# Moving 14 of 31 convolution shifts of the odd mixer from TensorE and VectorE to ScalarE and accumulating DMAs

## The chip, the cores and the metric

The kernel runs on one core of one Trainium2 chip. The metric is the device time of one execution in microseconds (us), the median of several runs.

## The reference, cut to what matters

A trunk of two layers on 512 tokens of width 1024, all in float32. Layer 0 has an attention mixer (even), layer 1 a mixer of a spatial gating unit and a causal convolution (odd):

```
for layer in 0, 1:
    h += 1/2 swiglu(rms(h));  h += Mixer_layer(rms(h));  h += 1/2 swiglu(rms(h))
    h += sigmoid(rms(h) @ ple_wgate[layer]) * (p[layer] @ ple_wproj[layer])     # p: 512 x 256, ple_wproj: 256 x 1024

odd mixer:
    zc, zd = split(xn @ w_in)                      # w_in: 1024 x 2048
    u, v = split(gelu(zc));  v = layer_norm(v)
    c_out = u * (block_mix(v) + bias)
    a, g = split(zd);  hd = a * sigmoid(g)         # 512 tokens x 512 channels
    y[t, c] = d_conv_b[c] + sum over shifts s = 0..30 of d_conv_w[30 - s, c] * hd[t - s, c]
    d_out = silu(layer_norm(y))
    mix = concat(c_out, d_out) @ w_out             # w_out: 1024 x 1024
```

## The kernel before

Activations are held with channels on the 128 partitions and the 512 tokens along the row, so one tile of 128x512 floats (256 KB) is a block of 128 channels. A big product is computed from two halves of each operand: a value is split into `hi` (a copy rounded to the type fp32r) and `lo` (what is left), and `mm3` makes three passes on TensorE, hi*hi, hi*lo, lo*hi. A plain `mm` on float32 tiles is one call that TensorE runs as several passes; the profile shows two rows for each call.

Weights come in units of 1 MB: SP issues the load into one of two `raw` buffers, ScalarE casts it to `whi` (L297), VectorE subtracts to get `wlo` (L321), and TensorE uses the pair.

Nothing is issued in the order of the code. Every operation is first recorded in a plan. `order()` then places them one by one with fixed costs for each operation, a bias for each stream of work (`CONV_BIAS`, `PP_BIAS` and so on: a larger bias makes a stream yield), and a limited number of buffers of each kind (`SLOTS`: 28 `a` buffers, 12 `t` buffers of 128x512) and of each kind in a stream (`CAPS`). What comes out is one fixed instruction sequence for each engine. On the chip each engine works its sequence off strictly in order, and waits at an instruction until its inputs and its buffer are ready.

The work of the odd mixer around the change, in `odd_mixer`: the products for `zd` give `hds`, four tiles of `hd` (ct = 0 to 3). Then the products for v, then those for u, run on TensorE; beside them VectorE works on the convolution. Of the 31 shifts, `PE_TAPS` = 4 are matmuls of `hds[ct]` with a diagonal matrix that ScalarE makes from the identity (stream `convp`), and the other 27 are `stt` operations on VectorE (L330), one for each shift and ct, that accumulate in `ys[ct]`. After the gating unit the first half of the product with w_out runs, and among its matmuls the tail of the convolution (`dtail`) starts: `mm(p, ones, ys[i])` sums the channels for the layer norm. The last half of w_out needs the normed `ys`.

`ple_proj(1)`, the product p[1] @ ple_wproj[1] for the end of layer 1, is also placed in the odd mixer (stream `pp`): 16 `mm` calls on float32, whose results are stored to DRAM (`pp<-t`) and read back at the end.

Of the kernel before, what the change touches and what calls it, by code (L numbers as in the profile page):

```python
# [257 lines left out]
def trunk(ctx: ExitStack, tc: tile.TileContext, A: dict, out: bass.AP):  # L258
# [89 lines left out]

    def gdma(o, x):
        P.op("POOL", 1000.0, lambda: nc.gpsimd.dma_start(ap(o), ap(x)), w=[o], r=[x, box.get("gate")], lat=2500.0)  # L350
# [32 lines left out]
    class Unit:  # L383


        def __init__(self, srcs, k, cols, by_cols):
            raw = P.tile("raw", (128, k, cols))
            for c0, c1, src in srcs:
                dma(raw[:, :, c0:c1], src, 0.5 * k * (c1 - c0))
            self.by_cols, self.half = by_cols, cols // 2 if by_cols else (k + 1) // 2  # L390
            h = self.half
            self.split([raw[:, :, h * i:h * (i + 1)] if by_cols else raw[:, h * i:h * (i + 1), :] for i in range(2)])
# [33 lines left out]
    def wunit(w, k0, k, c0, cols):  # L426
        src = w[128 * k0:128 * (k0 + k), c0:c0 + cols].rearrange("(k p) c -> p k c", p=128)
        return Unit([(0, cols, src)], k, cols, k == KD)
# [158 lines left out]
    def ffn(pre, layer, norm, nxt, hook=None, first=None):  # L587
        xs, rcol, rb = norm.finish()
        wg, wu, wd = A[pre + "_wg"][layer], A[pre + "_wu"][layer], A[pre + "_wd"][layer]
        for j0, j1 in ((0, 6), (6, 11)):  # L590
            cats = []
            for j in range(j0, j1):
# [5 lines left out]
                if hook is not None and j == 7:  # L598
                    box["gate"] = cats[-1][0]
                    with P.on("hook", HOOK_BIAS):  # L600
                        hook()
# [34 lines left out]
    def ple_proj(layer, after):  # L636
# [11 lines left out]
        for mg in range(2):  # L648
            wp = [at() for _ in range(2)]
            for k in range(2):  # L650
                dma(wp[k], A["ple_wproj"][layer, 128 * k:128 * k + 128, 512 * mg:512 * mg + 512], 256, after)
            for i in range(4):
                p = ps()
                for k in range(2):
                    x, y = (wp[k], pT[k]) if layer == 0 else (pT[k], wp[k])
                    mm(p, x[:, 128 * i:128 * i + 128], y, k == 0, k == 1)
                c = tt()
                acopy(c, p)
                d = dram_tile(f"pp{layer}{mg}{i}")
                dma(d, c, 256)  # L660
                kept.append(d)
# [111 lines left out]
    def even_mixer(norm, nxt, cos, sin):  # L773
# [198 lines left out]
        with P.on("pp", PP0_BIAS):  # L972
            box[0] = ple_proj(0, bqk[7])
# [85 lines left out]
    def odd_mixer(norm, nxt, consts):  # L1059
# [21 lines left out]
        with P.on("convp", CONVP_BIAS):  # L1081

            for ct in range(4):
                p = ps()
                for i in range(PE_TAPS):
                    dg = tt(shape=(128, 128))
                    act(dg, ident, AF.Copy, scale=cvw[:, 4 * (last - i) + ct:4 * (last - i) + ct + 1])
                    mm(p[:, i:S], dg, hds[ct][:, 0:S - i], i == 0, i == PE_TAPS - 1)
                y = at()
                act(y, p, AF.Identity, bias=vcol[:, 17 + ct:18 + ct])  # L1090
                ys.append(y)
        with P.on("conv", CONV_BIAS):
            for ct in range(4):
                y = ys[ct]
                for i in range(last - PE_TAPS, -1, -1):
                    sh = last - i
                    stt(y[:, sh:S], hds[ct][:, 0:S - sh], cvw[:, 4 * i + ct:4 * i + ct + 1], y[:, sh:S], OP.mult, OP.add)
# [111 lines left out]
    def odd_consts_hook():  # L1209
# [15 lines left out]
    ffn("ffn2", 1, n, m)  # L1225
# [11 lines left out]
TOPK_BIAS, AQ_BIAS, CONV_BIAS, CONVP_BIAS, PP_BIAS, DTAIL_BIAS, HOOK_BIAS, PE_TAPS = 2000, 450, 3000, -300, 200, -300, 400, 4  # L1237
PP0_BIAS = 600
PAD = 416
# [30 lines left out]
```

## Time and profile before

| | |
|---|---|
| median of 3 runs | 2010.78 us (2010.63 to 2011.23) |
| the profiled execution: its time, its span | 2010.54 us, 2008.6 us |
| TensorE (PE) busy | 1991.3 us, 99% of the span |
| VectorE (DVE) busy | 1080.8 us, 54% |
| ScalarE (ACT) busy | 723.2 us, 36% |
| GpSimd (POOL) busy | 13.8 us, 1% |
| granted TensorE clock | 0.999 |

The span runs from the first to the last instruction of the trace; 1.9 us of the execution's time lie outside it. Matmuls are pipelined, so the busy time of TensorE counts a matmul row until its modelled end; how long one takes when many follow each other is read from the starts of neighbouring rows. The odd mixer lies between 1428 and about 1604 us of the span.

### The profile page before, as it was taken

The numbers are of one execution on the slowest core, as the hardware profiler recorded it, in microseconds if no ns is written. First come the engines' busy times: TensorE is split into PE (matmuls) and PEld (weight loads), VectorE is DVE, ScalarE is ACT, GpSimd is POOL, SyncE is SP. The second block draws the span as 40 slices with busy tenths as digits, with TensorE's granted clock in tenths as the row PEclk, the third lists the DMA queues.
The fourth block names the chain that finished last, engine by engine and source line by source line (L and its number), as shares of the span: only waits on it lengthen the run. The fifth ranks groups of instructions, "written<-read, shape, count | busy, mean of one in ns | idle before, by whom it ended". The sixth has DMA issues, their size and how long they took to land.

```text
span 2008.6 us, 22735 instructions
## 1 busy us (share of the span) xinstructions
PE 1991.3 (99%) x9154; PEld 1630.2 (81%) x9154; DVE 1080.8 (54%) x1797; ACT 723.2 (36%) x1057; POOL 13.8 (1%) x35
## 2 busy tenths in 40 slices
PE   8999999999999999999999999999999999999999
PEld 7888888888767888888888888888767888888887
DVE  6442464489986544344466443444699744334443
ACT  6322233344756422132254222223425533213232
POOL 0000000000000000000000000000000000000000
PEclk9999999999999999999999999999999999999999
DMA  5323322354330323332233322323333232323222
GB/s 189 105 97 98 108 85 84 94 160 141 96 110 22 104 86 105 94 95 95 95 121 110 105 98 92 105 75 103 107 105 105 84 97 92 105 85 104 95 104 75
DMA packets 164778, 202.28 MB, mean 101 GB/s; under 512 B 9968, under 2 KB 123072, under 8 KB 164672
## 3 DMA queue, kind: packets, MB, share of 16 engines
q1 hardware_dynamic: 164016, 200.38, 31.3%
q8 instruction: 72, 1.18, 0.2%
q0 software_dynamic: 528, 0.41, 0.2%
q14 instruction: 34, 0.28, 0.0%
q10 hardware_dynamic: 128, 0.03, 0.0%
HBM read 185.33 MB, written 6.29 MB: 95 GB/s over the span
## 4 chain that ended last, share of the span: by engine, by line
PE 97%; DVE 1%; ACT 1%; DMA 1%; issue 0%; SPq 0%; ACTq 0%; DVEq 0%
PE ps L281 30%; PE ps L282 30%; PE ps L283 30%; PE ps L276 6%; PE ps L287 1%; DMA whi<-in_x_dram 0%; ACT t L292 0%; ACT t L297 0%; DVE t L962 0%; DVE t L330 0%; DVE wlo L330 0%; DMA t<-t 0%; DVE t L309 0%; DVE wlo L321 0%; DVE a L913 0%
## 5 line engine op out<-in xcount | busy, mean ns | idle before, releaser
L297 ACT CAST whi<-raw 128x1024 fp32r<-128x1024 f32 (+2 forms) x342 | 348.7, 1022 | 976.3 <-PE ps L282 936.7
L321 DVE TENSOR_TENSOR wlo<-raw,whi 128x1024 fp32r<-128x1024 f32 (+2 forms) x342 | 405.1, 1185 | 496.8 <-ACT whi L297 496.0
L281 PE MATMUL ps<-x,whi 128*128 128x512 f32 x1664 | 655.8, 394 | 0.6 <-ACT x L297 0.6
L282 PE MATMUL ps<-x,whi 128*128 128x512 f32 x1664 | 648.7, 390 | 0.6 <-DVE x L321 0.6
L283 PE MATMUL ps<-x,wlo 128*128 128x512 f32 x1664 | 648.8, 390 | 0.0
L281 PEld LDWEIGHTS ps<-x,whi 128*128 128x128 f32 x1664 | 313.1, 188 | 66.2 <-ACT x L297 1.1
L283 PEld LDWEIGHTS ps<-x,wlo 128*128 128x128 f32 x1664 | 312.9, 188 | 65.6
L282 PEld LDWEIGHTS ps<-x,whi 128*128 128x128 f32 x1664 | 313.2, 188 | 65.1 <-DVE x L321 1.2
L281 PE MATMUL ps<-a,whi 128*128 128x512 f32 x832 | 325.1, 391 | 0.0
L282 PE MATMUL ps<-a,whi 128*128 128x512 f32 x832 | 323.9, 389 | 0.0
L283 PE MATMUL ps<-a,wlo 128*128 128x512 f32 x832 | 323.8, 389 | 0.0
L281 PEld LDWEIGHTS ps<-a,whi 128*128 128x128 f32 x832 | 156.3, 188 | 32.8 <-issue 0.5
L283 PEld LDWEIGHTS ps<-a,wlo 128*128 128x128 f32 x832 | 156.2, 188 | 32.6
L282 PEld LDWEIGHTS ps<-a,whi 128*128 128x128 f32 x832 | 156.2, 188 | 32.3 <-DVE a L321 0.7
L315 DVE TENSOR_TENSOR t<-ps,t 128x512 f32<-128x512 f32 x88 | 60.8, 691 | 209.1 <-PE ps L283 208.3
L315 DVE TENSOR_TENSOR t<-ps,rb 128x512 f32<-128x512 f32 x100 | 68.7, 687 | 112.1 <-PE ps L283 109.9
L330 DVE SCALAR_TENSOR_TENSOR a<-a 128x508 f32<-128x508 f32 (+23 forms) x108 | 72.7, 731 | 5.0 <-ACT a L292 4.6
L292 ACT ACTIVATE t<-t 128x512 f32<-128x512 f32 x100 | 62.9, 629 | 22.9 <-DVE t L315 22.8
L297 ACT CAST a<-t 128x512 fp32r<-128x512 f32 x88 | 54.8, 623 | 36.8 <-DVE t L315 36.8
L315 DVE TENSOR_TENSOR t<-t,rb 128x512 f32<-128x512 f32 x92 | 63.2, 687 | 1.2
L321 DVE TENSOR_TENSOR a<-t,a 128x512 fp32r<-128x512 f32 x88 | 60.4, 686 | 5.2 <-ACT a L297 4.8
L276 PE MATMUL ps<-a 128*128 128x512 f32 (+3 forms) x152 | 58.6, 501 | 1.5 <-ACT t L297 0.5
(167 smaller groups left out, 1358.8 us busy)
## 6 DMA issues: line engine op xcount, KB each, us to landing
raw<-in_ffn_wg_dram SPq DMA_DIRECT2D x43, 1024.0 KB, 5.1
raw<-in_ffn_wu_dram SPq DMA_DIRECT2D x43, 1024.0 KB, 5.1
raw<-in_ffn_wd_dram SPq DMA_DIRECT2D x40, 1024.0 KB, 4.9
raw<-in_ple_wgate_dram SPq DMA_DIRECT2D x8, 1024.0 KB, 5.0
raw<-in_od_w_in_dram SPq DMA_DIRECT2D x8, 1024.0 KB, 5.5
raw<-in_ev_w_in_dram SPq DMA_DIRECT2D x7, 1024.0 KB, 5.8
raw<-in_ffn_wd_dram SPq DMA_DIRECT2D x8, 512.0 KB, 3.7
raw<-in_ev_w_out_dram SPq DMA_DIRECT2D x4, 1024.0 KB, 5.3
```

Of the source, the lines that this page charges most:

```text
L276: P.op("PE", cost, lambda: nc.tensor.matmul(ap(p), ap(a), ap(b), start=start, stop=stop), w=[p], r=[a, b], lat=160.0)
L281: nc.tensor.matmul(q, x, u, start=first, stop=False)
L282: nc.tensor.matmul(q, x, v, start=False, stop=False)
L283: return nc.tensor.matmul(q, y, u, start=False, stop=last)
L287: P.op("PE", 107.0, lambda: nc.tensor.transpose(ap(p), ap(x), ap(idn)), w=[p], r=[x, idn], lat=160.0)
L292: P.op("ACT", cost, lambda: nc.scalar.activation(ap(o), ap(x), func, scale=ap(scale), bias=ap(bias), **({"accum_out": ap(accum)} if accum ...
L297: P.op("ACT", 0.83 * o.n + (52.0 if x.psum else 93.0), lambda: nc.scalar.copy(ap(o), ap(x)), w=[o], r=[x])
L315: dve(o, lambda: nc.vector.tensor_mul(ap(o), ap(a), ap(b)), [a, b])
L321: dve(o, lambda: nc.vector.tensor_sub(ap(o), ap(a), ap(b)), [a, b])
L330: dve(o, lambda: nc.vector.scalar_tensor_tensor(ap(o), ap(a), ap(s), ap(b), op0=op0, op1=op1, **kw()), [a, s, b], extra=[accum] if accum i ...
```

## The change

The four matmul shifts are gone. Shifts 0 to 13 are now formed by ScalarE and added up by DMAs: `zs[ct]` starts as shift 0 with the bias, and for each shift 1 to 13 and each ct ScalarE writes `tp` = weight * shifted `hds[ct]`, and GpSimd issues a DMA that adds `tp` onto `zs[ct]` in place (`accum_op`). Shifts 14 to 30 stay on VectorE, in new tiles `ys` that start with a memset and a `tensor_scalar`. Four more accumulating DMAs add `zs` to `ys`. The product of `ple_proj(1)` becomes 16 `mm3`, with `p` and `ple_wproj` split into hi and lo as other operands are.

```diff
+    def added(o, x):
+        P.op("POOL", 1100.0, lambda: nc.gpsimd.dma_start(ap(o), ap(x), accum_op=OP.add), w=[o], r=[x], lat=2500.0)
...
+    def ple_proj(layer, after):
+        if layer == 0:
+            return ple_proj2(layer, after)
...
+        u = wunit(A["ple_wproj"][layer], 0, 2, 0, D, after)
...
+            pT.append((tt(F32R), tt(F32R)))
+            split_evac(pT[k], p)
...
-                    x, y = (wp[k], pT[k]) if layer == 0 else (pT[k], wp[k])
-                    mm(p, x[:, 128 * i:128 * i + 128], y, k == 0, k == 1)
+                    mm3(p, tok(pT[k], i), u.pick(k, 512 * mg, 512), k == 0, k == 1)
...
         with P.on("convp", CONVP_BIAS):
+            zs = [at() for _ in range(4)]
             for ct in range(4):
-                p = ps()
-                for i in range(PE_TAPS):
-                    dg = tt(shape=(128, 128))
-                    act(dg, ident, AF.Copy, scale=cvw[:, 4 * (last - i) + ct:4 * (last - i) + ct + 1])
-                    mm(p[:, i:S], dg, hds[ct][:, 0:S - i], i == 0, i == PE_TAPS - 1)
-                y = at()
-                act(y, p, AF.Identity, bias=vcol[:, 17 + ct:18 + ct])
-                ys.append(y)
+                act(zs[ct], hds[ct], AF.Identity, scale=cvw[:, 4 * last + ct:4 * last + ct + 1], bias=vcol[:, 17 + ct:18 + ct])
+            for sh in range(1, DMA_TAPS):
+                for ct in range(4):
+                    w1 = cvw[:, 4 * (last - sh) + ct:4 * (last - sh) + ct + 1]
+                    tp = tt()
+                    act(tp[:, 0:S - sh], hds[ct][:, 0:S - sh], AF.Copy, scale=w1)
+                    added(zs[ct][:, sh:S], tp[:, 0:S - sh])
         with P.on("conv", CONV_BIAS):
+            ys = [at() for _ in range(4)]
             for ct in range(4):
                 y = ys[ct]
-                for i in range(last - PE_TAPS, -1, -1):
-                    sh = last - i
-                    stt(y[:, sh:S], hds[ct][:, 0:S - sh], cvw[:, 4 * i + ct:4 * i + ct + 1], y[:, sh:S], OP.mult, OP.add)
+                for sh in range(DMA_TAPS, last + 1):
+                    w1 = cvw[:, 4 * (last - sh) + ct:4 * (last - sh) + ct + 1]
+                    if sh == DMA_TAPS:
+                        vset(y[:, 0:sh], 0.0)
+                        ts(y[:, sh:S], hds[ct][:, 0:S - sh], w1, None, OP.mult)
+                    else:
+                        stt(y[:, sh:S], hds[ct][:, 0:S - sh], w1, y[:, sh:S], OP.mult, OP.add)
+            for ct in range(4):
+                added(ys[ct], zs[ct])
...
-TOPK_BIAS, AQ_BIAS, CONV_BIAS, CONVP_BIAS, PP_BIAS, DTAIL_BIAS, HOOK_BIAS, PE_TAPS = 2000, 450, 3000, -300, 200, -300, 400, 4
+TOPK_BIAS, AQ_BIAS, CONV_BIAS, CONVP_BIAS, PP_BIAS, DTAIL_BIAS, HOOK_BIAS, DMA_TAPS = 2000, 450, 3000, 400, 200, -300, 400, 14
```

The caps change with it: stream `convp` may hold 5 `t` buffers (3 before), stream `pp` 7 (3 before); the projection of layer 0 keeps its old limits under the new name `pp0`.

Since `order()` decides the sequences, three places show what the edits move. The first is GpSimd's sequence. Before, it ended with four small memsets for the gating unit's tiles:

```order
L343 MEMSET whi_10821 128x1
L343 MEMSET wlo_10823 128x1
L343 MEMSET whi_10860 128x1
L343 MEMSET wlo_10864 128x1
L1266 UNCONDITIONAL_BRANCH
```

Now 56 DMAs stand among and behind them. Here a_10832, a_10862, a_10998 and a_11038 are `zs` of ct 0 to 3, and the `t` tiles are `tp`:

```order
L350 DMA a_10832<-t_10839 128x511
L343 MEMSET whi_10859 128x1
L343 MEMSET wlo_10867 128x1
L350 DMA a_10862<-t_10873 128x511
L350 DMA a_10998<-t_11005 128x511
L350 DMA a_11038<-t_11044 128x511
L350 DMA a_10832<-t_11058 128x510
L350 DMA a_10862<-t_11065 128x510
L350 DMA a_10998<-t_11072 128x510
L350 DMA a_11038<-t_11079 128x510
```

The DMAs go round the four ct, one round for each shift, 13 rounds, and a last round adds `zs` to `ys`. A DMA of one round writes the tile that the round before it wrote, and waits for that to land.

The second place is ScalarE's sequence, in the middle of the v products. whi_11157 is the second half of `ple_wproj`; the rows with 128x508, 128x507 and 128x506 write `tp` for shifts 4, 5 and 6:

```order
L292 ACTIVATE t_11141<-a_11023,a_10763 128x508
L292 ACTIVATE t_11152<-a_10827,a_10763 128x507
L297 CAST whi_11157<-raw_10992 128x1024
L292 ACTIVATE t_11165<-a_10852,a_10763 128x507
L292 ACTIVATE t_11173<-a_10990,a_10763 128x507
L292 ACTIVATE t_11185<-a_11023,a_10763 128x507
L292 ACTIVATE t_11196<-a_10827,a_10763 128x506
L297 COPY t_11204<-ps_11121 128x512
```

A cast of weights for TensorE now stands behind rows of `tp`, each of which waits for a `t` buffer that an earlier accumulating DMA has read; t_11152 waits for the DMA of ct 0 in round 3.

The third place is TensorE's sequence at the start of the convolution's tail, where ps_11664 to ps_11693 are sums of the w_out product, ones_73 is the matrix of ones, and a_186 and a_194 are `ys` of ct 0 and 1:

```order
L281 MATMUL ps_11664<-x_11673,whi_11481 128x512
L282 MATMUL ps_11664<-x_11681,whi_11481 128x512
L283 MATMUL ps_11664<-x_11673,wlo_11498 128x512
L276 MATMUL ps_11718<-a_186,ones_73 128x512
L281 MATMUL ps_11677<-x_11673,whi_11481 128x512
L282 MATMUL ps_11677<-x_11681,whi_11481 128x512
L283 MATMUL ps_11677<-x_11673,wlo_11498 128x512
L276 MATMUL ps_11718<-a_194,ones_73 128x512
```

These four matmuls with ones (one for each ct) now stand together behind the ninth product of w_out; before, three of them stood ahead of the gating unit's matmuls, as each `ys` was ready. The names a_186 and so on are low because the memsets of `ys` have no input: VectorE does them at the start of the program, and four of the 28 `a` buffers are held from there. In the even mixer this changes the order of some 60 `mm3` among about 250 small matmuls; behind that stretch the sequences are the same again up to the odd mixer.

## Rows read from the trace of the kernel before

**Rows 1.** The page: the span, busy time of each engine, the chain that ended last.

```profile
span 2008.6 us, 22735 instructions
PE 1991.3 (99%) x9154; PEld 1630.2 (81%) x9154; DVE 1080.8 (54%) x1797; ACT 723.2 (36%) x1057; POOL 13.8 (1%) x35
...
PE 97%; DVE 1%; ACT 1%; DMA 1%; issue 0%; SPq 0%; ACTq 0%; DVEq 0%
```

**Rows 2.** Windows: length, engines' busy us (instructions), PE clock, DMA share, GB/s.

```profile
480.00:575.00 95.00, 93.65 (x496) 70.90 (x494) 92.42 (x302) 62.38 (x142) 0.52 (x1) 1.00 0.43 125
...
1424.00:1604.00 180.00, 179.03 (x771) 136.03 (x770) 151.76 (x241) 78.78 (x116) 0.40 (x4) 0.99 0.30 100
...
1466.00:1532.00 66.00, 66.00 (x248) 45.46 (x247) 64.61 (x101) 25.15 (x38) 0.00 (x0) 1.00 0.33 112
```

**Rows 3.** Timeline of TensorE at the first convolution matmuls: start, duration, instruction.

```profile
1439.58 0.39 PE L283 MATMUL ps<-x,wlo 128*128 128x512 f32 x1
1439.81 3.59 PE L276 MATMUL ps<-a,t 128*128 128x512 f32 x8
1442.84 0.80 PE L281 MATMUL ps<-x,whi 128*128 128x512 f32 x1
1443.47 0.39 PE L282 MATMUL ps<-x,whi 128*128 128x512 f32 x1
1443.70 0.39 PE L283 MATMUL ps<-x,wlo 128*128 128x512 f32 x1
1443.92 0.39 PE L281 MATMUL ps<-x,whi 128*128 128x512 f32 x1
```

**Rows 4.** TensorE's groups by shape, 1424 to 1604 us: convolution and projection.

```profile
L276 PE MATMUL ps<-a 128*128 128x512 f32 x32 | 15.4, 592 | 0.0
...
L276 PE MATMUL ps<-a,t 128*128 128x512 f32 x8 | 4.1, 591 | 0.0
```

**Rows 5.** Timeline of VectorE when the last `hds` is written, and its shifts.

```profile
1469.66 3.95 DVE L330 SCALAR_TENSOR_TENSOR a<-a 128x491 f32<-128x491 f32 x6
1473.52 0.69 DVE L315 TENSOR_TENSOR a<-ps,t 128x512 f32<-128x512 f32 x1
```

**Rows 6.** ScalarE's groups by shape, 1424 to 1604 us.

```profile
L297 ACT CAST whi<-raw 128x1024 fp32r<-128x1024 f32 x24 | 25.1, 1049 | 37.4 <-PE ps L282 28.7 <-PE ps L283 5.6 <-issue 3.0
...
L292 ACT ACTIVATE x<-h,gcol 128x512 fp32r<-128x512 f32 x8 | 5.7, 714 | 6.6 <-DVE h L318 6.6
L292 ACT ACTIVATE t<-ident,a 128x128 f32<-128x128 f32 x16 | 5.2, 390 | 1.2 <-DVE a L334 1.2
```

**Rows 7.** Timeline of TensorE: the gating unit, and the w_out product behind it.

```profile
1473.06 0.39 PE L283 MATMUL ps<-x,wlo 128*128 128x512 f32 x1
...
1537.93 3.74 PE L276 MATMUL ps<-whi,a 128*128 128x128 f32 x32
1541.50 2.31 PE L287 MATMUL ps<-ident,wlo 128*128 128x128 f32 x16
1544.06 0.50 PE L281 MATMUL ps<-x,whi 128*128 128x512 f32 x1 [0.24 <-ACT x L297]
1545.11 0.50 PE L282 MATMUL ps<-x,whi 128*128 128x512 f32 x1 [0.56 <-DVE x L321]
```

**Rows 8.** Timeline of GpSimd: its one DMA of 128x512.

```profile
143.92 0.58 POOL L350 DMA_DIRECT2D t<-in_pos_dram  x1 [0.21 <-issue]
```

**Rows 9.** DMA issues of the whole run: KB each, median us from issue to landing.

```profile
raw<-in_od_w_in_dram SPq DMA_DIRECT2D x8, 1024.0 KB, 5.5
...
pp<-t SPq DMA_DIRECT2D x16, 256.0 KB, 2.4
...
t<-in_pos_dram POOLq DMA_DIRECT2D x1, 256.0 KB, 3.6
```

**Rows 10.** DMA queues, 100 to 160 us: packets, MB, share of 16 engines.

```profile
q0 software_dynamic: 368, 0.27, 2.3%
```

More of the change, by code (lines that the diff above doesn't have):

```diff
@@ L383, in trunk, with __init__ @@
     class Unit:
-        def __init__(self, srcs, k, cols, by_cols):
+        def __init__(self, srcs, k, cols, by_cols, after=None):
             raw = P.tile("raw", (128, k, cols))
             for c0, c1, src in srcs:
-                dma(raw[:, :, c0:c1], src, 0.5 * k * (c1 - c0))
+                dma(raw[:, :, c0:c1], src, 0.5 * k * (c1 - c0), after)
             self.by_cols, self.half = by_cols, cols // 2 if by_cols else (k + 1) // 2
@@ L424, in load, with wunit @@
             self.raw.append(r)
-    def wunit(w, k0, k, c0, cols):
+    def wunit(w, k0, k, c0, cols, after=None):
         src = w[128 * k0:128 * (k0 + k), c0:c0 + cols].rearrange("(k p) c -> p k c", p=128)
-        return Unit([(0, cols, src)], k, cols, k == KD)
+        return Unit([(0, cols, src)], k, cols, k == KD, after)
     ident = const_tile("ident", [128, 128])
@@ L599, in ffn @@
                     box["gate"] = cats[-1][0]
-                    with P.on("hook", HOOK_BIAS):
+                    with P.on("hook" if pre == "ffn1" else "pp", HOOK_BIAS if pre == "ffn1" else PP_BIAS):
                         hook()
@@ L634, in ple_mid, with ple_proj2 @@
                 nxt.stat(4 * j + s)
-    def ple_proj(layer, after):
+    def ple_proj2(layer, after):
         pT = [at() for _ in range(2)]
@@ L654, in ple_proj @@
                 for k in range(2):
-                    x, y = (wp[k], pT[k]) if layer == 0 else (pT[k], wp[k])
-                    mm(p, x[:, 128 * i:128 * i + 128], y, k == 0, k == 1)
+                    mm(p, wp[k][:, 128 * i:128 * i + 128], pT[k], k == 0, k == 1)
+                c = tt()
+                acopy(c, p)
+                d = dram_tile(f"pp{layer}{mg}{i}")
+                dma(d, c, 256)
+                kept.append(d)
+        return kept
+    def ple_proj(layer, after):
+        if layer == 0:
+            return ple_proj2(layer, after)
+        pT = []
+        ptok = [tt(shape=(128, 2, 256)) for _ in range(2)]
+        for i in range(2):
+            dma(ptok[i], A["p"][layer, 0, 256 * i:256 * i + 256, :].rearrange("(t p) d -> p t d", p=128), 256, after)
+        u = wunit(A["ple_wproj"][layer], 0, 2, 0, D, after)
+        for k in range(2):
+            p = ps()
+            for t in range(NT):
+                transpose(p[:, 128 * t:128 * t + 128], ptok[t // 2][:, t % 2, 128 * k:128 * k + 128], ident)
+            pT.append((tt(F32R), tt(F32R)))
+            split_evac(pT[k], p)
+        kept = []
+        for mg in range(2):
+            for i in range(4):
+                p = ps()
+                for k in range(2):
+                    mm3(p, tok(pT[k], i), u.pick(k, 512 * mg, 512), k == 0, k == 1)
                 c = tt()
@@ L970, in softmax_exp_ @@
             return es, sm
-        with P.on("pp", PP0_BIAS):
+        with P.on("pp0", PP0_BIAS):
             box[0] = ple_proj(0, bqk[7])
@@ L1224, in trunk @@
     m = Norm("ple_g", 1, at)
-    ffn("ffn2", 1, n, m)
+    ffn("ffn2", 1, n, m, None)
     ple_last(1, m, box[1])
@@ L1234 @@
         ("ps", "lgpvA"): 3, ("ps", "pvB"): 4, ("ps", "pvA"): 5, ("ps", "aq"): 2, ("ps", "sc"): 2, ("t", "lgpvB"): 6,
[2 rows of a table removed]
-TOPK_BIAS, AQ_BIAS, CONV_BIAS, CONVP_BIAS, PP_BIAS, DTAIL_BIAS, HOOK_BIAS, PE_TAPS = 2000, 450, 3000, -300, 200, -300, 400, 4
[2 rows of a table added]
+TOPK_BIAS, AQ_BIAS, CONV_BIAS, CONVP_BIAS, PP_BIAS, DTAIL_BIAS, HOOK_BIAS, DMA_TAPS = 2000, 450, 3000, 400, 200, -300, 400, 14
+PAD = 416
 PP0_BIAS = 600
-PAD = 416
 LG_BIAS, LGA_BIAS, PVA_BIAS, SIDE_BIAS, SC_BIAS = -100, -100, -300, 0, -200
```

4 rows, old and new, of the table CAPS are left out of this document.

## The prediction

> **What bounds the kernel now.** I read the page first. TensorE is busy 99% of the span, and it carries 97% of the chain that ended last [rows 1]. So a microsecond of TensorE's work that goes is a microsecond of the kernel, unless a wait comes in its place. Then I cut the span into windows. In the odd mixer, 1424 to 1604 us, TensorE idles 0.97 of 180 us, while VectorE has 151.8 us of work; between 1466 and 1532 us VectorE is full (64.6 of 66), TensorE has no gap, ScalarE works 25.2 us, and the DMA engines are taken for 0.33 of the time at 112 GB/s [rows 2]. VectorE is therefore nearly a second bound of this stage, GpSimd has nothing to do, and ScalarE and the DMA engines have room. The change uses that room. The question is whether a chain of dependent DMAs fits under TensorE's work.
>
> **What goes on TensorE.** The four matmul shifts of one ct start at 1439.81, and the second row of the next mm3 starts at 1443.47; taking off one pass, 0.227 us (1443.92 less 1443.70), leaves 3.43 us for four calls, 0.857 us a call [rows 3]. There are four ct: 4 x 3.43 = 13.7 us. The projection has 16 calls (32 rows of two a call) of the same shape [rows 4], 16 x 0.857 = 13.7 us. As 16 mm3 of three passes it costs 16 x 0.68 = 10.9 us, so 2.8 us go. The eight transposes of p stay. Together TensorE loses **16.5 us**.
>
> **What comes on ScalarE and VectorE.** Each `tp` is an activation of 128x512 with a scale for each partition, as the row of 0.714 us is; they follow each other at about 0.63 [rows 6]. 56 of them are 35 us, less the 16 diagonal tiles of 0.39 and four bias copies, and plus two casts of `ple_wproj` of 1.05 [rows 6]. In 1466 to 1532 us ScalarE would go from 25 to about 57 of 66 us: covered, but close. VectorE loses 11 `stt` for each ct (27 become 16, and a `tensor_scalar`), 44 of 0.66 us (3.95 for six) [rows 5], so 29 us, and gets about 4 us for splitting `ple_wproj` and p. It stops being full. That is worth nothing by itself, since TensorE had no gap there for VectorE to cause. Also at no price I count the five changed caps and biases, the four memsets at the start, and the reordered stretch of the even mixer: there TensorE idles 1.35 of 95 us and VectorE is full [rows 2], so by these rows the new order could give back 1.4 us or cost a few; I take zero.
>
> **The chain of DMAs.** Round 1 to 13 and the adding of `zs` to `ys` make 14 rounds of four DMAs, each waiting for the landing of the one four places before it. Call the time of a round R. Where does it start? The last `hds` is written at 1474.2 us [rows 5]; three of the four conv groups, 10.3 us, stood before that on TensorE, so it will be at 1463.9. ScalarE then needs four operations of about 0.6 us, and round 2 begins at about 1466.4. The last round, which begins 12 R later, has landed for ct 0 at 1466.4 + 13 R.
>
> When is it wanted? The gating unit's matmuls start at 1537.93 and the w_out products at about 1544.9 [rows 7]. Ahead of them go 16.5 us, and 2.6 us of three matmuls with ones that are moved behind (3 x 0.857). So w_out starts at 1525.8. Nine products later (6.1 us), at 1531.9, TensorE meets the first matmul with ones, which reads `ys` of ct 0. That gives **R up to 5.04 us** without a wait (5.2 by the last ct at 1535.8).
>
> ScalarE's order sets the same pace earlier. The cast of the second half of `ple_wproj` stands behind the `tp` that needs round 3 of ct 0 landed, 1466.4 + 2 R. With R = 4.6 the cast ends at 1477.3 and its `wlo` at 1478.5. TensorE's zd products end at 1463.0 (1473.3 [rows 7] less 10.3), and it wants that half 24 places later (0.9 us of transposes, 23 products), at 1479.5. So a late chain holds ScalarE, ScalarE holds the casts, and TensorE waits once, not twice, for the same lateness.
>
> How long is R? No row of before shows an accumulating DMA. From below: four issues of 0.58 us [rows 8] are 2.3 us, and a 256 KB store from SP lands in 2.4 us [rows 9]. The one GpSimd DMA of this shape lands 3.6 us after its issue [rows 9]. By throughput, 112 GB/s at a share of 0.33 is 339 GB/s for all engines, so 256 KB take 0.77 us and four 3.1; beside the other traffic 3.1 / 0.67 = 4.6 us. From above: on GpSimd's queue 0.27 MB took 2.3% of 60 us, 1.4 us of all 16 engines [rows 10], which makes a round 5.5 us alone and 8 beside the other traffic; if an accumulation also takes the engines twice, more. I take R = 4.6: it is what the transfers of this very stage show, and it holds the landing of 3.6. Then nothing waits at 1531.9, with 5.7 us to spare.
>
> **The sum.** The profiled execution took 2010.54 us, 0.24 below the median. 2010.5 - 16.5 = 1994.0. I add 1.5 us for new short waits of the size of the 0.97 us that this stage has [rows 2], since the gating unit loses the matmuls with ones that filled its gaps, and forecast **1995.5 us**.
>
> **Rivals.** First, the chain is somewhat late, R between 5.04 and 6: each tenth of R costs 1.3 us. At R = 5.6 the wait is 7.3 us and the time 2003. Two values of the trace speak for it, the upper engine time and the 86% load of ScalarE, through which every `tp` must pass in order.
>
> Second, and on the other side: **an accumulation takes the DMA engines twice**, since it reads its destination as well as its source before it writes. Then a DMA costs 1.54 us of all engines. 52 of them (rounds 2 to 14) are 80 us, and other traffic of the stage, 0.33 of 66 us, another 22 us. The chain ends at 1466.4 + 102 = 1568, 36.5 us late, and the kernel takes 2010.5 - 16.5 + 36.5 + 1.5 = 2032 us. The point from which it decides is R = 6.3 (5.04 + 16.5 / 13): above that the change loses. For it speaks that the transfer needs three passes over memory where a copy has two; against it that the engines' share counts busy time that may overlap. The Trainium skill, "Collectives: The Full Stack", section "The bandwidth ceiling: the fold count and why AG ≠ RS ≠ AR", says that a reducing transfer reads two sources on one ring and so runs at half the rate of a copy (32 against 62 GB/s there). By that rule this rival holds and the time would be about 2032. No row here shows an accumulation, so the trace neither agrees nor disagrees; I give it weight because the bounds of R, taken without it, already reach 5.5 to 8.
>
> Third, the gain is eaten exactly: R near 6.3, or the 16.5 us spent on several short waits; 2007 to 2015 us.
>
> Fourth, the four lost `a` buffers disturb the even mixer. VectorE is the bound of that stretch and its own work is unchanged, so I put it at two or three times the 1.35 us that it idles now, 3.5 us: 1999 us.
>
> **How the numbers follow.** 4 us, 0.2%, is about what a measurement of this kernel can tell from no change. The chain fits (with or without a small price in the even mixer): 0.45, 1992 to 2000. Late with a gain left: 0.15, 2000 to 2006.5. Eaten up: 0.10. Slower, by the second rival or by the upper engine time: 0.30, from 2015 to 2060 with most of it below 2032. So faster 0.60, same 0.10, slower 0.30. The forecast is the likeliest case's. The range is 1992 to 2030, which leaves out about 0.05 below and 0.15 above; the likeliest case alone has 1992 to 2000.
>
> **What the profile after would show.** Right: the odd mixer 15 to 17 us shorter, no fp32 matmuls with diagonals, TensorE's gaps in it still around 1 to 3 us, GpSimd DMAs that land 3 to 4.5 us after issue, rounds of 4 to 5 us. Wrong by size: a gap of TensorE released by ScalarE's casts or by the matmul with ones, and DMAs on POOL's queue in a spacing of more than 1.3 us for the whole chain. Wrong in kind: DMA share near 1 from 1466 us on, weight loads that land in far more than 5.5 us [rows 9], or a POOL instruction of much more than 0.58 us. Idle time of TensorE in 480 to 575 us well above 1.35 would show the even mixer's price.

## The result, and the profile after

| | before | after |
|---|---|---|
| median | 2010.7 us (2010.54 to 2011.23, 4 runs) | 2032.36 us (2031.62 to 2034.4, 4 runs) |
| ratio | | 1.0109 [1.0091, 1.0126] |
| span of the profiled execution | 2008.6 us | 2029.8 us |

The changed kernel is 21.7 us (1.1%) slower, which is clear of the noise; forecast were 1995.5 us and a range up to 2030. The second rival had given 2032.

The page of the kernel after, span, engines, chain that ended last and GpSimd's DMA queue [for before: rows 1]:

```profile
span 2029.8 us, 22869 instructions
...
PE 1986.2 (98%) x9138; PEld 1633.5 (80%) x9138; DVE 1061.2 (52%) x1770; ACT 751.8 (37%) x1090; POOL 62.7 (3%) x91
...
q0 software_dynamic: 8592, 14.90, 4.2%
...
PE 93%; ACT 2%; DMA 2%; DVE 2%; issue 1%; POOL 0%; ACTq 0%; DVEq 0%; POOLq 0%
```

TensorE's busy time fell by only 5.1 us although 16.5 us of work went, and its share of the chain fell from 97 to 93%. To find the place, take two marks that both programs have, the four transposes at the opening of the odd mixer and of layer 1's second ffn in the chain of waits: before 1428.48 and 1607.45, after 1431.49 and 1628.07 us. So 3.0 us are lost ahead of the odd mixer, 17.6 in it (196.58 for 178.97), and 0.6 behind it, together the 21.2 of the span. The windows of the kernel after, with the columns of [rows 2]: the even mixer, the odd mixer from mark to mark, and its middle in four parts:

```profile
480.00:575.00 95.00, 92.90 (x488) 70.20 (x487) 92.63 (x293) 58.60 (x131) 2.60 (x5) 1.00 0.43 128
1431.49:1628.07 196.58, 170.97 (x745) 137.89 (x744) 127.40 (x202) 107.04 (x152) 49.39 (x60) 0.92 0.71 168
...
1470.00:1490.00 20.00, 18.06 (x71) 14.21 (x70) 16.14 (x26) 12.68 (x18) 11.45 (x13) 0.91 1.07 223
1490.00:1530.00 40.00, 36.16 (x156) 28.60 (x155) 25.32 (x42) 29.94 (x45) 15.75 (x18) 1.00 1.06 242
1530.00:1560.00 30.00, 17.90 (x78) 14.51 (x76) 16.02 (x28) 17.71 (x26) 13.66 (x16) 0.79 1.06 230
1560.00:1600.00 40.00, 32.27 (x139) 25.32 (x140) 16.78 (x29) 14.62 (x20) 4.65 (x6) 0.82 0.38 81
```

And the same stretch from mark to mark in the kernel before:

```profile
1428.48:1607.45 178.97, 178.00 (x761) 135.07 (x760) 150.27 (x238) 77.95 (x114) 0.40 (x4) 0.99 0.31 104
```

Read the DMA share (the last column but one): 0.31 before, above 1.0 from 1470 to 1560 after. The share sums the times of packets over 16 engines, so above 1 some of these times overlap; read it as full. TensorE stands idle 25.6 us (196.58 less 170.97), 0.97 before. Its work should have fallen from 178.0 to 161.5; it was busy 170.97, so 9.5 us more went into running the same matmuls at the granted clock of the last-but-two column (0.79 and 0.82 in the two late windows, 1.00 in the middle). In sum -16.5 + 24.6 + 9.5 = 17.6. The 9.5 is what is left over, but the clock itself gives nearly as much: TensorE's busy time times (1 less the granted clock), summed over windows of half a microsecond, is 9.8 us in this stage after and 1.7 before.

The waits of TensorE in the odd mixer of the kernel after (line <- releaser: us in total, times, longest):

```profile
PE ps L276 <- DMA a<-a: 12.9, 1, 12.9
PE ps L276 <- DVE whi L318: 3.5, 2, 2.9
PE ps L281 <- ACT t L297: 3.4, 3, 1.6
PE ps L287 <- DVE wlo L330: 2.3, 2, 1.9
```

Half of the idle time is one wait, for `a<-a`, the accumulation of `zs` onto `ys`. The chain of waits of the kernel after at that place (start, us, what):

```profile
1553.99 1.06 ACT whi L297
1555.05 0.34 issue
1555.40 6.87 DMA a<-t
...
1562.80 4.80 DMA a<-a
1567.59 0.14 issue
1567.73 2.04 PE ps L276 x2
```

The accumulation of shift 13 for ct 0 is issued at 1555.40 and ends 6.87 us later; only then can the `a<-a` of ct 0 be issued, which ends at 1567.6, and the first matmul with ones starts. GpSimd's timeline of the kernel after, at the first of the four DMAs of round 2 and at the last round:

```profile
1470.17 2.65 POOL L350 DMA_DIRECT2D a<-t  x3 [0.23 <-ACT t L292]
...
1555.40 0.87 POOL L350 DMA_DIRECT2D a<-t  x1 [0.88 <-ACT whi L297]
1557.11 0.87 POOL L350 DMA_DIRECT2D a<-t  x1 [0.84 <-DMA a<-t]
...
1562.80 0.87 POOL L350 DMA_DIRECT2D a<-a  x1 [0.72 <-DMA a<-t]
```

Twelve rounds lie between 1470.17 and 1562.80: R = 7.7 us, where 4.6 was taken and 6.3 was the break-even. Transfers of others are held up too; issues of the kernel after between 1424 and 1640 us (KB each, median us to landing), with the queue's share:

```profile
q0 software_dynamic: 8064, 14.50, 37.5%
...
raw<-in_od_w_out_dram SPq DMA_DIRECT2D x4, 1024.0 KB, 9.6
...
pp<-t SPq DMA_DIRECT2D x8, 256.0 KB, 5.9
...
a<-t POOLq DMA_DIRECT2D x4, 254.0 KB, 8.3
```

37.5% of 216 us over 56 DMAs is 1.45 us of all 16 engines for each; `pp<-t` had landed in 2.4 [rows 9].

### The profile page after: what moved, and what is told of

Read it like the earlier page. It is cut to its first block, busy times and chain, and to the rows that moved or that the text cites. A ratio compares the mean times of both kernels' runs of the same rounds, so it can differ in the third digit from the quotient of the medians.

```text
span 2029.8 us, 22869 instructions
## 1 busy us (share of the span) xinstructions
PE 1986.2 (98%) x9138; PEld 1633.5 (80%) x9138; DVE 1061.2 (52%) x1770; ACT 751.8 (37%) x1090; POOL 62.7 (3%) x91
## 4 chain that ended last, share of the span: by engine, by line
PE 93%; ACT 2%; DMA 2%; DVE 2%; issue 1%; POOL 0%; ACTq 0%; DVEq 0%; POOLq 0%
PE ps L281 29%; PE ps L282 29%; PE ps L283 29%; PE ps L276 5%; PE ps L287 1%; ACT t L292 1%; DMA a<-t 1%; DMA pp<-t 1%; ACT whi L297 1%; DMA x<-t 0%; DVE wlo L321 0%; DMA a<-a 0%; ACT t L297 0%; DMA whi<-in_x_dram 0%; ACT L292 0%
## 5 line engine op out<-in xcount | busy, mean ns | idle before, releaser
L297 ACT CAST whi<-raw 128x1024 fp32r<-128x1024 f32 (+2 forms) x344 | 351.6, 1024 | 970.9 <-PE ps L282 920.4
L297 ACT CAST a<-t 128x512 fp32r<-128x512 f32 x88 | 55.0, 625 | 36.3 <-DVE t L315 36.3
L330 DVE SCALAR_TENSOR_TENSOR h<-ps,h 128x512 f32<-128x512 f32 x64 | 42.6, 689 | 14.1 <-PE ps L283 14.1
L297 ACT COPY t<-ps 128x512 f32<-128x512 f32 (+3 forms) x54 | 27.7, 524 | 56.6 <-PE ps L283 35.6
```

What stands on the lines that cost most here:

```text
L297: P.op("ACT", 0.83 * o.n + (52.0 if x.psum else 93.0), lambda: nc.scalar.copy(ap(o), ap(x)), w=[o], r=[x])
L330: dve(o, lambda: nc.vector.scalar_tensor_tensor(ap(o), ap(a), ap(s), ap(b), op0=op0, op1=op1, **kw()), [a, s, b], extra=[accum] if accum i ...
```

## The experiments

"Stage" is the odd mixer from mark to mark, "idle" TensorE's idle time in it, "work" what its matmuls take at the clock of the kernel before (178.0 less what the kernel leaves out: 0.857 us a call, 2.8 us for the new projection), "clock" the rest of its busy time. These four are of the one profiled execution, whose time lay up to 3.3 us off the median (e1 2013.99, e7 2036.19, e5 2028.76 us). Summed from the granted clock as above, less the 1.7 of before, the clock's part comes out within 1.4 us of this column in every row. The ratio is to the kernel before, run beside each (2010.7 to 2012.2 us); its interval is 2 to 4 us to either side, and a smaller difference between two rows is not clear of the noise.

| kernel | time us | ratio to before | stage | work | idle | clock |
|---|---|---|---|---|---|---|
| before | 2010.7 | | 179.0 | 178.0 | 1.0 | |
| after | 2032.36 | 1.0109 [1.0091, 1.0126] | 196.6 | 161.5 | 25.6 | 9.5 |
| e1 plain copies | 2010.76 | 0.9991 [0.9978, 1.0004] | 179.4 | 161.5 | 10.7 | 7.2 |
| e2 half the columns | 2015.11 | 1.0013 [0.9995, 1.003] | 179.0 | 161.5 | 12.3 | 5.3 |
| e3 two sums | 2040.78 | 1.0149 [1.0119, 1.0178] | 202.8 | 161.5 | 34.0 | 7.4 |
| e5 memsets late | 2031.53 | 1.0099 [1.0085, 1.0113] | 195.8 | 161.5 | 26.5 | 7.8 |
| e6 ten shifts | 2012.81 | 1.0005 [0.9995, 1.0016] | 180.6 | 161.5 | 11.7 | 7.4 |
| e7 other costs in the plan | 2033.2 | 1.0106 [1.0088, 1.0125] | 204.0 | 161.5 | 29.6 | 12.9 |
| e8 projection alone | 2019.95 | 1.0046 [1.0032, 1.0059] | 187.1 | 175.2 | 8.2 | 3.7 |
| e9 convolution alone | 2035.98 | 1.0121 [1.0104, 1.0138] | 200.6 | 164.3 | 29.9 | 6.5 |
| e10 the same, copies | 2008.0 | 0.9978 [0.9964, 0.9992] | 173.4 | 164.3 | 3.9 | 5.2 |
| e14 the same, late memsets | 2005.58 | 0.9969 [0.9957, 0.9982] | 173.9 | 164.3 | 8.9 | 0.7 |
| e11 2 shifts TensorE, 4 DMA | 2012.5 | 1.0002 [0.9993, 1.0011] | 178.5 | 171.1 | 4.4 | 3.0 |
| e12 1 TensorE, 6 DMA | 2003.25 | 0.9957 [0.9943, 0.9972] | 171.1 | 167.7 | 3.3 | 0.0 |
| e13 0 TensorE, 6 DMA | 2009.51 | 0.9996 [0.9987, 1.0005] | 177.3 | 164.3 | 8.4 | 4.6 |
| e15 e13 and new projection | 2018.03 | 1.0034 [1.0021, 1.0046] | 186.2 | 161.5 | 15.2 | 9.5 |

Four theories, as the expectations name them. A: the accumulations' throughput sets R, because the DMA engines are full. B: it is the turn of a single DMA that waits for the one before it. C: it is GpSimd's issuing, 0.87 us and a gap of 0.4 for each DMA, 5 us a round. D: the plan's order is at fault. The edits below are shortened to the calls that they change.

**e1, plain copies.** The same DMAs without the adding.

```diff
-nc.gpsimd.dma_start(ap(o), ap(x), accum_op=OP.add)
+nc.gpsimd.dma_start(ap(o), ap(x))
```

> The 56 DMAs of GpSimd copy instead of adding (the sum over shifts 0 to 13 is left out, the result is not the reference's); every wait, tile and place in the order stays. Theory A, an accumulation takes the DMA engines twice as long as a copy (1.46 us of all 16 against about 0.77) and the engines are full: the share of the engines between 1470 and 1560 us falls from 1.05 to about 0.6 to 0.8, a round from 7.7 us to about 5, and the kernel takes 1998 to 2008 us. Theory B, the chain is as long as it is because each DMA waits for the landing of the one four places before it, whatever the landing costs the engines: a round stays at 7 us or more and the time at 2025 to 2035 us. Theory C, GpSimd's issuing (0.87 us and a gap of 0.4) is the limit: a round stays at 5 us or more and only what lies above 5 us goes.

21.6 us came back. The queue's row of this kernel, 1424 to 1640 us:

```profile
q0 software_dynamic: 3648, 14.50, 16.9%
```

The same bytes take 0.65 us of all engines for each DMA instead of 1.45, the DMA share from 1470 to 1560 fell to 0.73, and R to 5.9 (round 2 at 1469.69, the adding of `zs` at 1540.83). That is Theory A, but the time stayed 3 us above its range: the gain that had been forecast is not there. What holds the chain then is in part ScalarE, through which every product passes. Its busy time in this window (the fourth engine of the row) is 36.92 of 40 us:

```profile
1490.00:1530.00 40.00, 35.88 (x175) 29.67 (x174) 29.29 (x53) 36.92 (x54) 13.14 (x25) 1.00 0.80 283
```

Between 1470 and 1541 us GpSimd waits 25.4 us for ScalarE and 17.0 for a DMA. e8 to e14 look for the rest.

**e2, half the columns** of each accumulation, the rest left out.

```diff
-dma_start(ap(o), ap(x), accum_op=OP.add)
+dma_start(ap(o)[:, 0:o.n // 2], ap(x)[:, 0:o.n // 2], accum_op=OP.add)
```

> All 56 DMAs accumulate, but only over the left half of their columns (the right half of the sum is left out, the result is not the reference's): same number, same waits, half the bytes. Theory A: 0.73 us of the engines for each, the engines are no longer full, a round of about 5 us, 1998 to 2008 us. Theory B: time to landing hardly depends on bytes, so a round stays near 7 us and the time above 2020 us. Theory C: as many issues, so a round of 5 us; together with A it would be near 2000 us, alone it says nothing of the rest.

The queue's row of this kernel in the same window:

```profile
q0 software_dynamic: 8064, 7.24, 21.9%
```

As many packets and half the bytes: 0.85 us for each DMA, and 17 us of the time. So the price goes mostly with the bytes. R was 6.0 and the time lay between the ranges of A and B. Theory C falls here, by GpSimd's timeline:

```profile
1479.34 8.05 POOL L350 DMA_DIRECT2D a<-t  x9 [2.56 <-ACT t L292]
```

Nine accumulations are issued in 8.05 us, 0.9 us each or 3.6 a round, well under the R of 7.7 and of 6.0 here.

**e3, two sums**: odd shifts go into a second set of tiles, so each DMA waits for the eighth before it, not the fourth. Four more DMAs join the sums.

```diff
+z2 = [at() for _ in range(4)]
-added(zs[ct][:, sh:S], tp[:, 0:S - sh])
+added((zs, z2)[sh % 2][ct][:, sh:S], tp[:, 0:S - sh])
```

> Odd shifts are added up in a second set of four tiles, even shifts in the first, and both are added to ys at the end (60 DMAs instead of 56, the same result): each DMA now waits for the landing of the one eight places before it. Theory A: the engines are full anyway, so the chain ends no sooner; four more DMAs of 1.46 us make it 2 to 8 us later: 2030 to 2042 us. Theory B: half the waiting for each shift, rounds of 4 us, the chain ends before it is wanted: 1996 to 2008 us. Theory C: a round of 5 us: 1998 to 2012 us.

It became slower, within the range of Theory A. An issue row of this kernel, 1433 to 1636 us:

```profile
a<-t POOLq DMA_DIRECT2D x4, 254.0 KB, 12.2
```

With twice as many under way each takes about half as long again (8.3 us in the kernel after, 12.2 here), and the DMA share stays above 1.0. Theory B falls: the engines are full, and a shorter dependence only lengthens the queue.

**e4 and e16, the DMAs by themselves**, at the end of the kernel before, with nothing beside them.

```diff
+for d in dsts: nc.gpsimd.dma_start(d, x)                    # copies
+for d in dsts: nc.gpsimd.dma_start(d, x, accum_op=OP.add)   # accumulations
+for d in dsts: nc.vector.tensor_copy(d, d)                  # starts as each lands
```

> The kernel before, and at its end, beside no other traffic, four groups of GpSimd DMAs of 128x512 floats between tiles in SBUF: 8 copies to eight tiles, 8 accumulations onto eight tiles, 4 copies onto one tile and 4 accumulations onto one tile, each waiting for the last. Theory A: 8 independent accumulations take the engines about 12 us against 6 for the copies, and set their spacing. Theory B: they end as soon as the copies, and an accumulation that waits for the last takes 6 us or more even alone. Theory C: both groups are spaced by GpSimd's issue, 1.2 us or more.

VectorE's timeline in e4: its copies start as one DMA after the other lands, first plain ones, then accumulations:

```profile
2014.14 0.43 DVE L1246 COPY iz<-iz 128x512 f32<-128x512 f32 x1 [0.19 <-DMA iz<-ix]
2014.76 0.43 DVE L1246 COPY iz<-iz 128x512 f32<-128x512 f32 x1 [0.19 <-DMA iz<-ix]
2015.38 0.43 DVE L1246 COPY iz<-iz 128x512 f32<-128x512 f32 x1 [0.19 <-DMA iz<-ix]
...
2022.02 0.43 DVE L1246 COPY iz<-iz 128x512 f32<-128x512 f32 x1 [1.01 <-DMA iz<-ix]
2023.41 0.43 DVE L1246 COPY iz<-iz 128x512 f32<-128x512 f32 x1 [0.96 <-DMA iz<-ix]
2024.85 0.43 DVE L1246 COPY iz<-iz 128x512 f32<-128x512 f32 x1 [1.01 <-DMA iz<-ix]
```

A copy of 256 KB every 0.62 us, an accumulation every 1.4 (1.35 on average up to the last, at 2030.11). One after another, each waiting for the last, a copy took 2.5 us from issue to issue (2034.20, 2036.70, 2039.19) and an accumulation 3.5 (2042.85, 2046.39, 2049.88). A round of four accumulations is then about 5.5 us by throughput, longer than the turn of 3.5. But a copy went in packets of 4 KB and an accumulation in packets of 2 KB, hence e16, where the rows of a second pair of groups are cut in two pieces of 1 KB.

```diff
+group([d[:, :, 0:256] for d in g], y[:, :, 0:256], False)
+group([d[:, :, 0:256] for d in g], y[:, :, 0:256], True)
```

> The kernel before with four groups of six GpSimd DMAs of 256 KB at its end, nothing beside them: copies and accumulations between plain tiles of 128x512, and both between tiles whose rows are cut in two pieces of 1 KB with a gap. In the earlier run alone a copy went in 64 packets of 4 KB and took 0.61 us, an accumulation in 128 packets of 2 KB and took 1.38 us: the time doubled, but so did the packets. If the doubled traffic is what costs (the destination is read too), the cut copies stay near 0.61 us and the cut accumulations near 1.4, though they have more packets. If it is the number of packets, the cut copies take 1.4 us or more, and the cut accumulations as much as those copies.

Packets, MB and share of the queue over each accumulating group of e16, of 11 us with whole rows and of 11.9 us with cut ones:

```profile
q0 software_dynamic: 864, 1.57, 79.6%
...
q0 software_dynamic: 1632, 1.57, 83.9%
```

Nearly twice the packets cost an accumulation 1.36 to 1.49 us (2031.47 to 2038.28 and 2043.20 to 2050.65, five each). The cut copies still went in packets of 4 KB, so that half of the test came to nothing. The packets an accumulation has more than a copy (144 and 80) are half of those added here, so by that they explain under 0.1 of the 0.75 us between the two.

**e5, memsets late**: the first writes of `ys` wait for `hds`, so that no `a` buffer is held from the start.

```diff
-vset(y[:, 0:sh], 0.0)
+vset_after(y[:, 0:sh], 0.0, hds[ct])
```

> The changed kernel, with the four memsets of ys placed after hds in the plan, so that no a buffer is held from the start. If the 3.0 us that are lost before the odd mixer (the matmuls that open it stand at 1431.5 instead of 1428.5 us) come from the four held buffers, they come back: the opening at 1428.5 and 2029 us in all. If they come from something else, the opening stays at 1431.5 and the time at 2032.

The even mixer's time returned: from a mark before it (four transposes of the same kind) to its end 276.99 us (386.92 to 663.91), 279.92 in the kernel after, 276.78 before. So the four lost buffers cost 3.1 us in the kernel after. The price varies: in the other kernels that hold them from the start (e1, e2, e3, e9, e10) this stretch takes 279.5 to 283.9 us, in all that do not 276.8 to 277.7. The odd mixer did not change, and of the 3 us the median shows 0.8, which is within the noise.

**e6 and e7, other counts and costs.** e6 moves ten shifts instead of 14 and tells the plan a longer DMA; e7 does the second alone. Both have e5's memsets.

```diff
-P.op("POOL", 1100.0, ... lat=2500.0)
+P.op("POOL", 1700.0, ... lat=4500.0)
-DMA_TAPS = 14
+DMA_TAPS = 10
```

> As e5_late, with shifts 0 to 9 instead of 0 to 13 by ScalarE and DMAs, VectorE takes 21 shifts, and the plan counts 1.7 us on GpSimd and 4.5 us to landing for an accumulation. Theory A (the engines' time per accumulation): 10 rounds of 7.0 to 7.7 us end at 1536 to 1544 us instead of 1570; about the time at which the tail is wanted: 1996 to 2006 us. If the chain is not what costs the time, but ScalarE's load and order (theory D): ScalarE has 16 products less, but the casts still stand behind waiting ones: 2008 to 2020 us.

> As e5_late with 14 shifts, only the plan's costs of an accumulation are those of e6 (1.7 and 4.5 us), so that casts and other work are placed for a slow chain. Theory A: the chain still needs 14 rounds of 7 us or more, TensorE's 21.8 us of other products cannot hide it, and the wait only moves to the matmuls with ones: 2020 to 2032 us. Theory D (the order placed ScalarE's casts behind products that wait): most of the loss goes, 1996 to 2010 us.

Sixteen DMAs fewer gave back 19 us. But 2012.8 us lies in the range that the expectation gave to Theory D, not in A's, so e6 alone does not decide. e7 does: the other plan alone gave nothing, and TensorE's wait for `a<-a` was 16.3 us instead of 12.9. Theory D falls as the cause of the loss. In e6 TensorE still waits 6.1 us for VectorE at the gating unit and 4.0 for `a<-a`.

**e8, the projection alone** in the kernel before: 16 `mm3` in place of 16 fp32 calls.

> The kernel before with the projection of layer 1 as mm3 alone; the convolution stays as before. By the sum of the prediction 2.8 us less: 2008 us, a ratio of 0.9986. If the split of ple_wproj and p and the buffers that it takes cost what it saves: no change.

It costs 8 to 9 us, where 2.8 less or no change was expected. TensorE's waits in this kernel's odd mixer (before: 0.97 us in all):

```profile
PE ps L276 <- DVE a L330: 2.6, 1, 2.6
PE ps L281 <- ACT a L297: 2.3, 1, 2.3
PE ps L287 <- DVE s L330: 1.5, 1, 1.5
PE ps L276 <- DVE whi L318: 1.0, 1, 1.0
```

The first is for the shifts on VectorE (L330), whose sum is late when TensorE wants it. VectorE was nearly full before, 87.1 of 90 us from 1470 to 1560; now it has 4.5 us more to do in the stage (154.78 for 150.27), and it waits 3.9 us for ScalarE's casts between 1490 and 1560, 0.5 before. How much each of the two costs is not told apart.

**e9, e10 and e14, the convolution alone** (the old projection); e10 with plain copies, e14 with late memsets too. Both of these leave out the sum over the first 14 shifts.

```diff
-                    mm3(p, tok(pT[k], i), u.pick(k, 512 * mg, 512), k == 0, k == 1)
+                    mm(p, x[:, 128 * i:128 * i + 128], y, k == 0, k == 1)
```

> The changed kernel with the projection of layer 1 as it was before (16 fp32 calls): the convolution's part of the change alone. If the parts add as forecast, the projection's 2.8 us are missing and the time is about 2035. If the one-pass products cost this stage something, as they did alone (about 8 us more than before), the time is about 2024. If the late chain is the only thing that TensorE waits for, the projection lies ahead of the wait and its length is hidden by it: 2032, unchanged.

> As the run before it, with plain copies in place of the 52 accumulations (the sum over the first 14 shifts is left out). It asks where the 11 to 16 us are that the plain copies did not give back beside the new projection. If the projection took them: about 1998 to 2001 (2011 less 13.7, and a few us for the even mixer's order and short waits). If ScalarE's load and the transfers beside the other traffic took them: about 2011 again.

> Changed kernel with all three suspects out: plain copies (the sum over the first 14 shifts is left out), the old projection, and the four memsets behind the hds. If the three account for the whole loss, the odd mixer stays at about 173 us, the even mixer returns to its time of before, and the run takes about 2003: 2010.8 less 13.7 and 6 for ScalarE's pace and the slower clock behind its gap. If something else of the change costs, it stays at 2008.

Beside the late chain the new projection is worth 3.6 us in the medians (e9 less after), near the 2.8 of the forecast but hardly clear of the noise. Beside copies it costs 6 us in the stage of the profiled executions and 2.8 in the medians (e1 less e10), which is within the noise. e14 came out at 2005.6, between the two times that were expected. The even mixer has its old time there, and one wait over 1 us is left:

```profile
PE ps L276 <- DMA a<-a: 8.2, 1, 8.2
PE ps L287 <- DVE wlo L330: 0.6, 1, 0.6
```

Even as copies the DMAs end too late. R is 5.1 there (from 1467.3, the second of three issues in a row from 1466.70, to 1528.25); the `a<-a` of ct 0 then lands in 6.9 us, at 1535.1, while this kernel's plan has TensorE at the matmuls with ones at 1526.95. Ahead of that the chain of waits runs over ScalarE, busy 9.97 and 9.82 us of the two stretches of 10 from 1500 to 1520.

**e11, e12, e13 and e15, a short chain.** Some shifts stay on TensorE, a few go to ScalarE and accumulations, VectorE adds the two sums, the old projection.

```diff
+        PE_TAPS, DMA_N = 1, 6          # e12; 2, 4 in e11; shift 0 by one activation and 1 to 6 by ScalarE in e13
...
-                for i in range(last - PE_TAPS, -1, -1):
+                for i in range(last - PE_TAPS - DMA_N, -1, -1):
...
+                tadd(ys[ct][:, PE_TAPS:S], ys[ct][:, PE_TAPS:S], zs[ct][:, PE_TAPS:S])
```

> Shifts 0 and 1 on TensorE as before, 2 to 5 by ScalarE and 12 accumulations, 25 on VectorE, the partial sums added by VectorE, the old projection. 12 accumulations at 1.46 us are 17.5 us of the DMA engines, long over before the sum is wanted at about 1530. By the throughput theory nothing waits for them: 2010.8 less 6.9 (8 calls of 0.857) and about 1 to 2 for waits, 2005. If ScalarE's added work or any accumulation in this stage is what costs, it gains nothing: 2011 or more.

> The same with one shift on TensorE, six by ScalarE and 20 accumulations, 24 on VectorE. 20 at 1.46 us are 29 us of the DMA engines, by which the chain ends near 1500 to 1510, still ahead of the sum. Throughput theory: 2010.8 less 10.3 and 1 to 2 us for waits, 2002. If weight loads held up by full DMA engines are what costs: above the run with 12, 2008 to 2015.

> The run with six DMA shifts and one on TensorE, with that last one gone to ScalarE as well: shift 0 by one activation into the sum, shifts 1 to 6 by ScalarE and 20 accumulations, 24 on VectorE, the old projection. 3.43 us of TensorE go. If the 20 accumulations stay covered: 2003.3 less 3.4, 2000. If VectorE, at 38.97 of 40 us between 1490 and 1530 in that run, or ScalarE now sets the pace, nothing is gained: 2003 to 2006.

> The first of these three with the new projection of layer 1. As forecast it takes 2.8 us less than that one, 1997. If the two casts and the splits on VectorE cost as they did in the kernel before, where VectorE had no room either, it takes 5 to 9 us more, 2005 to 2009.

e12 beats both kernels, as expected: 7.9 us less than before. The window of its odd mixer, and then all of TensorE's waits in it:

```profile
1429.65:1600.71 171.06, 167.72 (x738) 130.72 (x736) 144.35 (x230) 88.84 (x126) 17.81 (x24) 0.99 0.49 139
```

```profile
PE ps L282 <- DVE x L321: 1.7, 1, 1.7
PE ps L276 <- DVE whi L318: 1.1, 1, 1.1
PE ps L287 <- DVE wlo L330: 0.6, 2, 0.3
```

Twelve calls of TensorE went (10.3 us); busy is 167.72, just 178.0 less 10.3, and no DMA is waited for: its last accumulation is issued at 1499.43. e11 lost what it saved to two waits for a load of `ple_wproj` (2.2 us, landing 9.8 us after issue where 5.8 was usual) and to the clock. In e13 TensorE idles 4.1 us between 1560 and 1600, behind ScalarE (`a`, L297, 2.8 us) and VectorE; it has the same 20 accumulations as e12, less work for TensorE, and takes 6 us more, above both times that were expected. Why is open. e15 confirms e8: against e13 the projection costs 8.5 us, where VectorE keeps 24 of the shifts.

## Why the prediction was wrong

**The step that failed is the choice of R.** "I take R = 4.6: it is what the transfers of this very stage show" carried the rate of plain transfers over to accumulations. Measured were 1.4 us alone where a copy takes 0.62, 1.45 us of all engines in the stage where 0.77 was used, and R = 7.7. R = 4.6 was too low for copies as well: with these it was 5.9 (e1) and 5.1 (e14), above the 5.04 that the sum allowed, with ScalarE nearly full, which was the other reason of the first rival. The text had the deciding values itself: 6.3 as the break-even, and 5.5 to 8 as what the GpSimd queue's row gave [rows 10]. That row was of small packets (0.27 MB in 368), and was put aside for a row that was nearer in bytes but of another operation. That its 1.4 us is also the price of an accumulation is chance.

**The second rival was right in kind**, as far as the runs can tell: it said 1.54 us for each DMA (1.45) and a DMA share near 1 (1.06). e16 leaves little for the packets. The Trainium skill, "Collectives: The Full Stack", section "The bandwidth ceiling: the fold count and why AG ≠ RS ≠ AR", says of transfers round a ring of three or more cores that a reducing step reads two sources on one ring and runs at about half the rate of a copy. The trace, of one core, agrees with that factor: the copies and the accumulations by themselves stand at 0.62 and 1.4 us. The Trainium skill, "DMA: Bandwidth & Descriptors", section "Rules for kernel authors", says that an accumulating DMA reads its destination and writes it later; no view here shows that read by itself, so why an accumulation costs twice is not shown.

**That its numbers fit so closely is partly luck.** It had the chain end at 1568 (1567.6), but the chain began 3.8 us later than said (1470.17 for 1466.4), most of it from the even mixer, and ran 4.6 us shorter (97.4 for 102). It had one wait of 36.5 us. The loss came to 35.1 us, but in three parts: 12.9 us at that place, 12.7 in other waits ahead of it, and 9.5 by the clock, which the rival did not have. And 2032 us had nothing for the even mixer, where 3.0 us went. That TensorE does not pay twice for the same lateness, though ScalarE is held as well, came out: 35 us in all, where the chain ended 35.7 us after 1531.9, the time at which TensorE was to want it.

**16.5 us of TensorE's work** were right as work: the stage has 745 rows where it had 761 (64 of fp32 calls gone, 48 of `mm3` come), and e12 got back what its calls were priced at.

**The projection's part, -2.8, was wrong outside the late chain:** its work on VectorE was counted as covered, in a stage from which 29 us of VectorE's shifts go. Where these shifts stay on VectorE, all or most, it costs 8 to 9 us (e8, e15). Beside the copies, where VectorE has room, it still costs 6 us in the stage of one execution each; e1 and e10 do not settle which order or wait does that.

**The even mixer at zero** was wrong by 3.0 us; the fourth rival had 3.5, and e5 shows its cause, the four buffers. **The clock** was not in the sum at all: 9.5 us. **Small waits**, 1.5 us, were as much as 12.7 (25.6 less 12.9). TensorE waited there for ScalarE and VectorE. ScalarE had itself waited 11.7 us for accumulations and 5.5 for the stores `pp<-t` between 1466 and 1532 us; how much of the 12.7 goes back to that is not told apart.

The medians go down as follows, one step at a time from after: accumulations to copies -21.6 (e1), old projection -2.8 (e10), late memsets -2.4 (e14), 2005.6 us. The first step is far above the noise; the other two are so only together, if barely. With the old projection the forecast would be 1998.3; the other 7.3 are about the wait of 8.2 that e14 still shows, with R = 5.1 instead of 4.6 and a last landing of 6.9 us instead of 3.6.

ScalarE stayed below what was forecast in 1466 to 1532 us, 48.6 of 66 us for 57: it was held by the chain, in the 11.7 us of waits just named.

## What to carry to other kernels

An idle DMA path is priced by the operation that goes there, not by the transfers that are there already: an accumulation took 2.2 times a copy's time by itself, and one look at two groups of eight at a kernel's end would have told. When a chain has a deadline and the price is open, count how many links fit at the upper price and move only these: 20 accumulations gave 8 us (e12), 40 with the new projection nothing (e6), 56 lost 22. A chain that fits is not yet a gain: 12 (e11) and the same 20 with another plan (e13) gave nothing, by waits elsewhere. Before an edit on the bound engine is taken as a gain, look which engine is second in that stage and what the edit gives it: the projection took 2.8 us of work from TensorE, gave VectorE 4.5 us and ScalarE two casts more, and left the kernel 8 to 9 us slower (e8).

## What the runs showed of the hardware

- An accumulating DMA of 256 KB from one on-chip tile to another takes 1.35 to 1.4 us of all DMA engines (1.49 with rows cut in two), a copy 0.62; its turn, one waiting for the other, is 3.5 us, a copy's 2.5. GpSimd's issuing instruction takes 0.87 us, a copy's 0.54.
- In and behind a wait TensorE's granted clock fell to its lower level for a while: 0.50 in 1560 to 1565 us, where it did nothing, and in the rows from 1570.00 to 1570.85 matmuls of 128x512 start 0.42 us apart, 1.2 GHz, where they start 0.23 apart at 2.4. It also fell where nothing was waited for: in the kernel before it was 0.50 from 1565 to 1568 us, shortly behind 32 matmuls of one column each (3.63 us from 1560.20). In the table, the kernels with over 8 us of idle time lose 3.7 to 12.9 us more by the clock, e14 only 0.7; e10, with 3.9 us idle, loses 5.2 (its clock was 0.50 from 1535 to 1544 us, behind a wait of 2.4). So the loss does not go by the idle time alone. Timeline of TensorE of the kernel after:

```profile
1567.73 2.04 PE L276 MATMUL ps<-a,ones 128*128 128x512 f32 x2 [12.87 <-DMA a<-a]
...
1570.00 0.63 PE L282 MATMUL ps<-x,whi 128*128 128x512 f32 x1
1570.42 0.63 PE L283 MATMUL ps<-x,wlo 128*128 128x512 f32 x1
1570.85 2.04 PE L276 MATMUL ps<-a,ones 128*128 128x512 f32 x4
1572.33 0.79 PE L281 MATMUL ps<-x,whi 128*128 128x512 f32 x1
1572.96 0.39 PE L282 MATMUL ps<-x,whi 128*128 128x512 f32 x1
1573.18 0.40 PE L283 MATMUL ps<-x,wlo 128*128 128x512 f32 x1
```
